# Gate and up of the layer-1 feed-forwards by Strassen's seven products, with all sums on VectorE

## Chip, core and metric

The kernel runs on one core of a Trainium2 chip. The metric is the device time of one execution in microseconds (us). Its engines are TensorE (PE, with weight loads shown as PEld), VectorE (DVE), ScalarE (ACT), GpSimd (POOL) and SyncE (SP, which only issues transfers here). All engines run at once, each through its own instructions in order; semaphores tie them together.

## The reference

One inference step of a trunk of two layers, in float32, for 528 prompt tokens (512 and 16 meta tokens) and 8 sample tokens, that is 536 columns. The width is 1024 and the feed-forward has 2816 hidden units:

```python
def swiglu(h, w_gu, w_down):
    gate, up = jnp.split(h @ w_gu, 2, axis=-1)
    return (jax.nn.silu(gate) * up) @ w_down
...
for l in range(DEPTH):
    xp = xp + 0.5 * swiglu(rmsnorm(xp, norm_g[l, 0]), ffn1_w_gu[l], ffn1_w_down[l])
    ...
    xp = xp + mp
    xs = xs + ms
    xp = xp + 0.5 * swiglu(rmsnorm(xp, norm_g[l, 2]), ffn2_w_gu[l], ffn2_w_down[l])
```

Here mp and ms are the mixer's outputs for the rows normalised with norm_g[l, 1]; the samples xs go through the feed-forwards as the prompt xp does. The mixer of layer 0 is a convolution module beside windowed attention; that of layer 1 is a grouped complex state-space model (SSM) with a gated linear projection (glu).

## The kernel before

Activations lie with the model width on the partitions: eight residual tiles `x[0]` to `x[7]` of [128, 536], in two halves of 268 columns (264 prompt tokens and 4 samples). Every product is made from exact parts: a factor is split into a high part, rounded to the format in which PE takes four-byte numbers in one pass, and the low part that is left. `weights` (L116 and on) loads a [128, 8, 128] block into `raw` (four buffers) on SP's queue, ACT copies it to `whi` (L126) and DVE subtracts to get `wlo` (L127), three buffers each. `gemm` (L137, L140) runs whi x xh, whi x xl and wlo x xh for eight rows of tiles and two halves: 48 matmuls of 268 columns.

`ffn` takes the 22 tiles of the hidden width in blocks of 8, 8 and 6. For each tile there are a gate product and an up product, 96 matmuls, into PSUM tiles `mm` and `S`. Then DVE scales gate by `R`, the reciprocal root mean square (L273), ACT takes silu (L274), DVE scales up (L275) and multiplies (L276), and ACT and DVE split the outcome into `mh` and `ml` (L146, L147). After a block the down products follow, eight of 48 (or 36) matmuls, each added to its residual tile by DVE (L288). In the last block `finalize` also makes the scaled parts `xh` and `xl` of each residual tile for the next stage (L155, L156) and adds up its squares (L162, L163); `rstd` sums the squares over the partitions by a product with ones (L185) and takes the root (L172 to L177).

The preparation of the SSM, `ssm_prep`, needs no token. It is a generator of 54 steps, one of which is drawn after each tile of the feed-forward up to the last two of a block, and after each of the first six down products: 34 steps lie in the second feed-forward of layer 0 and 20 in the first of layer 1. Its steps hold DVE work (L736 to L742, L898 to L905), some small products, ACT copies (L889, L923) and transfers to scratch on POOL's queue. The order on each engine is made by a scheduler from the dependences and the order in the program, so an engine's row is not simply the program's.

## Time and profile before

| | |
|---|---|
| time, median of 3 runs | 2066.57 us (2066.05 to 2070.46) |
| span of the profiled execution | 2071.1 us (its time around the span isn't told apart) |
| PE busy | 2023.6 us, 98% |
| DVE busy | 1133.5 us, 55% |
| ACT busy | 644.8 us, 31% |
| chain that ended last | PE 91%, DVE 5% |
| mean granted clock of PE | 0.989 of full |

By stage the profiled execution divides so: load of tokens and first feed-forward up to 262 us, mixer of layer 0 to 665, its second feed-forward to 1058, first feed-forward of layer 1 to 1450, SSM mixer to 1560, glu to 1675, second feed-forward of layer 1 with the end to 2071. In the page "idle before" a group of operations is the time its engine stood still ahead of them, with the one that ended it. A group's mean is over the whole span unless a stretch is named.

### The profile page before, as it was taken

To read this page: it belongs to the slowest core of one execution; us is meant where nothing else is said; L and a number is where in the kernel's file an instruction comes from. 1 tells how busy PE (TensorE), PEld (TensorE's weight loads), DVE (VectorE), ACT (ScalarE), POOL (GpSimd) and SP (SyncE) were. 2 spreads that over 40 slices of the span, in tenths; PEclk is the share of its full clock that TensorE was granted. 3 is DMA by queue.
4 is the path that set the end of the run, shared out by engine and by line. 5 is a ranking of instruction groups with operands and counts; after the bars stand their busy time and mean duration, and the time that the engine had idled before them with its cause. 6 is when DMAs were issued, how large, how long until landed. Compare 5 with 4: busy or idle time off the path is not lost.

```text
span 2071.1 us, 37762 instructions
## 1 busy us (share of the span) xinstructions
PE 2023.6 (98%) x16302; PEld 1981.4 (96%) x16302; DVE 1133.5 (55%) x1819; ACT 644.8 (31%) x970; POOL 114.4 (6%) x172
## 2 busy tenths in 40 slices
PE   6999999999999999999999999999989999999998
PEld 5999999998779999999999999999989999999998
DVE  4443434479967874655575544345784444344336
ACT  3322222333446322322242222123324332122223
POOL 2000000012200000000010000000110000000000
PEclk9999999999979999999999999999999999999999
DMA  6432332232005343344344433623682323332321
GB/s 174 113 100 84 91 92 86 79 84 52 27 19 129 112 129 92 105 122 115 97 133 121 119 109 109 181 81 91 185 256 77 92 87 88 92 92 83 91 77 57
DMA packets 371494, 213.51 MB, mean 103 GB/s; under 512 B 36119, under 2 KB 362323, under 8 KB 370921
## 3 DMA queue, kind: packets, MB, share of 16 engines
q1 hardware_dynamic: 354897, 190.63, 32.1%
q0 software_dynamic: 5872, 19.40, 3.1%
q8 instruction: 128, 2.10, 0.4%
q10 hardware_dynamic: 10560, 1.09, 0.4%
q14 instruction: 37, 0.30, 0.0%
HBM read 193.14 MB, written 23.65 MB: 105 GB/s over the span
## 4 chain that ended last, share of the span: by engine, by line
PE 91%; DVE 5%; DMA 1%; ACT 1%; issue 1%; SPq 1%; ACTq 0%; DVEq 0%
PE mm L137 39%; PE mm L140 19%; PE S L137 18%; PE S L140 9%; DVE yc L425 1%; PE S L598 1%; DVE wlo L127 1%; DMA raw<-in_ffn_w_gu 1%; PE ms L606 0%; PE ms L887 0%; DMA mC<-dC 0%; PE ms L612 0%; DVE Sc L1029 0%; SPq L203 0%; PE ms L919 0%
## 5 line engine op out<-in xcount | busy, mean ns | idle before, releaser
L126 ACT ACTIVATE whi<-raw 128x1024 fp32r<-128x1024 f32 (+2 forms) x324 | 329.5, 1017 | 1138.9 <-PE mm L137 533.5
L137 PE MATMUL mm<-xh,whi 128*128 128x268 f32 x2144 | 445.2, 289 | 7.4 <-DVE tb L406 2.6
L137 PE MATMUL mm<-xl,whi 128*128 128x268 f32 x2144 | 442.1, 287 | 0.0
L140 PE MATMUL mm<-xh,wlo 128*128 128x268 f32 x2144 | 441.6, 287 | 0.0
L127 DVE TENSOR_TENSOR wlo<-raw,whi 128x1024 fp32r<-128x1024 f32 (+2 forms) x324 | 381.1, 1177 | 67.7 <-ACT whi L126 59.8
L137 PEld LDWEIGHTS mm<-xh,whi 128*128 128x128 f32 x2144 | 335.0, 189 | 10.2 <-DVE tb L406 3.0
L137 PEld LDWEIGHTS mm<-xl,whi 128*128 128x128 f32 x2144 | 336.2, 189 | 1.1 <-issue 0.5
L140 PEld LDWEIGHTS mm<-xh,wlo 128*128 128x128 f32 x2144 | 335.1, 188 | 2.0 <-issue 1.7
L137 PE MATMUL mm<-mh,whi 128*128 128x268 f32 x1216 | 258.6, 290 | 1.9 <-DVE xl L156 1.1
L140 PE MATMUL mm<-mh,wlo 128*128 128x268 f32 x1216 | 256.3, 287 | 0.8 <-DVE wlo L127 0.8
L137 PE MATMUL mm<-ml,whi 128*128 128x268 f32 x1216 | 256.4, 288 | 0.0
L137 PE MATMUL S<-xh,whi 128*128 128x268 f32 x1024 | 212.3, 288 | 2.6 <-DVE us L985 2.6
L137 PE MATMUL S<-xl,whi 128*128 128x268 f32 x1024 | 210.3, 287 | 0.0
L140 PE MATMUL S<-xh,wlo 128*128 128x268 f32 x1024 | 210.1, 287 | 0.0
L137 PEld LDWEIGHTS mm<-mh,whi 128*128 128x128 f32 x1216 | 193.2, 190 | 3.5 <-ACT whi L126 2.1
L140 PEld LDWEIGHTS mm<-mh,wlo 128*128 128x128 f32 x1216 | 192.9, 189 | 1.5 <-DVE wlo L127 1.0
L137 PEld LDWEIGHTS mm<-ml,whi 128*128 128x128 f32 x1216 | 193.7, 190 | 0.4 <-issue 0.2
L137 PEld LDWEIGHTS S<-xh,whi 128*128 128x128 f32 x1024 | 160.4, 189 | 3.1 <-issue 2.9
L137 PEld LDWEIGHTS S<-xl,whi 128*128 128x128 f32 x1024 | 160.6, 189 | 0.1
L140 PEld LDWEIGHTS S<-xh,wlo 128*128 128x128 f32 x1024 | 160.0, 189 | 0.0
L275 DVE TENSOR_TENSOR tb<-mm,R 128x536 f32<-128x536 f32 x60 | 43.0, 717 | 193.5 <-PE mm L140 193.1
L288 DVE SCALAR_TENSOR_TENSOR x<-mm,x 128x536 f32<-128x536 f32 x59 | 42.2, 716 | 163.1 <-PE mm L140 163.1
(455 smaller groups left out, 2203.3 us busy)
## 6 DMA issues: line engine op xcount, KB each, us to landing
raw<-in_ffn_w_gu SPq DMA_DIRECT2D x174, 512.0 KB
raw<-in_ffn_w_down SPq DMA_DIRECT2D x64, 512.0 KB
raw<-in_ffn_w_down SPq DMA_DIRECT2D x32, 384.0 KB
raw<-in_ssm_w_glu SPq DMA_DIRECT2D x16, 512.0 KB
raw<-in_ab_w_in SPq DMA_DIRECT2D x10, 512.0 KB
dC<-CL POOLq DMA_DIRECT2D x32, 128.0 KB, 3.0
dB<-B POOLq DMA_DIRECT2D x8, 512.0 KB, 3.5
dT<-dK POOLq DMA_DIRECT2D x8, 512.0 KB, 4.9
```

The source lines that it names most:

```text
L126: nc.scalar.activation(hi[:, :K], raw[:, :K], AF.Copy)
L127: nc.vector.tensor_sub(lo[:, :K], raw[:, :K], hi[:, :K].bitcast(F32))
L137: nc.tensor.matmul(ps[:, h, :HT], hi[:, k, :], src[:, h * HT:(h + 1) * HT], start=(k == 0 and i == 0), stop=False)
L140: nc.tensor.matmul(ps[:, h, :HT], lo[:, k, :], xh[k][:, h * HT:(h + 1) * HT], start=False, stop=(k == K - 1))
L275: nc.vector.tensor_mul(halves(b[:]), pu[:, :, :HT], R)
L288: nc.vector.scalar_tensor_tensor(x, ps[:, :, :HT], 0.5, x, op0=OP.mult, op1=OP.add)
L425: nc.vector.scalar_tensor_tensor(y, z, wcol(c, j), y, op0=OP.mult, op1=OP.add)
L598: nc.tensor.matmul(S[:, g, :w], qT[t][rw, 128 * b:128 * b + 128], kT[rw, k0:k0 + w], start=False, stop=True)
```

## The change

In the two feed-forwards of layer 1, gate and up of a tile are computed together. The input is seen as two halves of the width (tiles 0 to 3 and 4 to 7) by two halves of the tokens, the weights as two halves of the width by gate and up, and the two-by-two product of blocks is made by the seven products of Strassen in Winograd's form. Each product P1 to P7 is 4 rows of tiles x 3 parts = 12 matmuls of 268 columns, so 84 for a tile where there were 96.

- `operands` (called by `finalize` for the input of these two feed-forwards) makes the sums of input blocks and splits each into parts: `xh`, `xl` hold scaled tiles or differences, `eh`, `el` and `fh`, `fl` further combinations.
- `seven_weights` loads gate (G) and up (U), makes the sums S, q and G + U with DVE (L230, L231, L233, L235 of the changed kernel) and splits G, U, S and the half-sized q: ACT at L226, DVE at L227. `DMASUM` is off.
- `seven` orders the products by the table `SLOTS`, so that products of two neighbouring tiles alternate. PSUM sums the products that share a bank; the rest goes by ACT copies out of PSUM (sn at L272 and L278, u3 at L280, tb at L284) and DVE sums of 268 columns (L276, L281, L286). Then come R, silu, R, the product and the split (L287 to L290, L148, L149).
- The SSM preparation, and that of mixer 0, is drawn two steps at a slot, so that the SSM's lies wholly in the second feed-forward of layer 0. `then` closes its pool and opens the pool `fx` of the new tiles ahead of the last down products; `glu` becomes a function of its own, so that `fx` can be opened between the SSM mixer and glu.

The removed comments are left out of the diff.

```diff
+SLOTS = dict(P1=0, P2=1, P6=3, P5=5, P7=6, P4=9, P3=11)
+STRASSEN, DMASUM = (3, 5), False
...
-        if g < 6:
+        if g in STRASSEN:
+            self.operands(d, col)
+        elif g < 6:
...
+    def extra(self, pool):
+        self.fx = pool
+        t = lambda n, w: pool.tile([128, w], F32R, name=n)
+        self.eh, self.el = ([t(f"{n}{k}", NT) for k in range(4)] for n in ("eh", "el"))
+        self.fh, self.fl = ([t(f"{n}{k}", HT) for k in range(4)] for n in ("fh", "fl"))
+    def operands(self, d, col):
+        nc, k = self.nc, d % 4
+        x, l, r = self.x[d], slice(0, HT), slice(HT, NT)
+        t = lambda n, bufs=1: self.fx.tile([128, NT], F32, name=n, bufs=bufs)
+        if d < 4:
+            if d == 0:
+                self.b12 = [self.fx.tile([128, HT], F32, name=f"b12{i}") for i in range(4)]
+                self.t1 = [self.fx.tile([128, NT], F32, name=f"t1{i}") for i in range(4)]
+            w, b = self.t1[k], self.b12[k]
+            nc.scalar.activation(w[:, l], x[:, l], AF.Copy, scale=col)
+            nc.scalar.activation(b[:], x[:, r], AF.Copy, scale=col)
+            nc.vector.tensor_sub(w[:, r], w[:, l], b[:])
+            self.put(self.xh[d][:], self.xl[d][:], w[:])
+            return
+        w, b = self.t1[k], self.b12[k]
+        u, e, f = t("ou"), t("oe"), self.fx.tile([128, HT], F32, name="of")
+        nc.scalar.activation(u[:], x[:], AF.Copy, scale=col)
+        self.put(self.xh[d][:], self.xl[d][:], u[:])
+        nc.vector.scalar_tensor_tensor(e[:, l], w[:, r], -1.0, u[:, r], op0=OP.mult, op1=OP.subtract)
+        nc.vector.tensor_sub(e[:, r], u[:, r], b[:])
+        self.put(self.eh[k][:], self.el[k][:], e[:])
+        nc.vector.scalar_tensor_tensor(f[:], e[:, l], -1.0, u[:, l], op0=OP.mult, op1=OP.subtract)
+        self.put(self.fh[k][:], self.fl[k][:], f[:])
+    def seven_weights(self, gu, f):
+        nc = self.nc
+        k0, k1 = slice(0, 4), slice(4, 8)
+        G, gh, gl = self.wtiles()
+        U, uh, ul = self.wtiles()
+        S = self.fx.tile([128, 8, 128], F32, name="sraw")
+        sh, sl = (self.wts.tile([128, 8, 128], F32R, name=n, bufs=3) for n in ("whi", "wlo"))
+        q = self.fx.tile([128, 4, 128], F32, name="sq4")
+        qh, ql = (self.fx.tile([128, 4, 128], F32R, name=n) for n in ("qh", "ql"))
+        g, u = gu[:, :, f:f + 128], gu[:, :, D_FF + f:D_FF + f + 128]
+        nc.sync.dma_start(G[:], g)
+        if DMASUM:
+            nc.sync.dma_start(S[:, k1], u[:, k1])
+            nc.sync.dma_start(U[:], u)
+            nc.gpsimd.dma_start(S[:, k1], u[:, k0], accum_op=OP.add)
+            nc.gpsimd.dma_start(U[:, k0], g[:, k0], accum_op=OP.add)
+        else:
+            nc.sync.dma_start(U[:], u)
+        def split(h, l, r):
+            nc.scalar.activation(h[:], r[:], AF.Copy)
+            nc.vector.tensor_sub(l[:], r[:], h[:].bitcast(F32))
+        split(gh, gl, G)
+        if not DMASUM:
+            nc.vector.tensor_add(S[:, k1], U[:, k0], U[:, k1])
+        nc.vector.tensor_add(S[:, k0], S[:, k1], G[:, k0])
+        split(sh, sl, S)
+        nc.vector.tensor_add(q[:], S[:, k0], G[:, k1])
+        if not DMASUM:
+            nc.vector.tensor_add(U[:, k0], U[:, k0], G[:, k0])
+        split(uh, ul, U)
+        split(qh, ql, q)
+        l, r = slice(0, HT), slice(HT, NT)
+        X = lambda t, c: [a[:, c] for a in t]
+        x0, x1 = slice(0, 4), slice(4, 8)
+        return {"P1": (gh, gl, 0, X(self.xh[:4], l), X(self.xl[:4], l)),
+                "P2": (gh, gl, 4, X(self.xh[4:], l), X(self.xl[4:], l)),
+                "P3": (qh, ql, 0, X(self.xh[4:], r), X(self.xl[4:], r)),
+                "P4": (uh, ul, 4, X(self.fh, l), X(self.fl, l)),
+                "P5": (sh, sl, 4, X(self.xh[:4], r), X(self.xl[:4], r)),
+                "P6": (sh, sl, 0, X(self.eh, l), X(self.el, l)),
+                "P7": (uh, ul, 0, X(self.eh, r), X(self.el, r))}
+    def seven(self, gu, f0, nf):
+        nc = self.nc
+        l, r = slice(0, HT), slice(HT, NT)
+        st, zs = {}, None
+        for n, p in sorted(((n, p) for n in range(nf) for p in SLOTS), key=lambda a: 7 * a[0] + SLOTS[a[1]]):
+            if p == "P1":
+                if n % 2 == 0:
+                    zs = self.scores()
+                w = self.seven_weights(gu, (f0 + n) * 128)
+                st[n] = dict(w=w, xy=self.acc2(), z=zs[:, n % 2], sn=self.fx.tile([128, NT], F32, name="sn", bufs=2),
+                             u3=self.fx.tile([128, HT], F32, name="u3"), a=self.work("ta"), b=self.work("tb"))
+            s = st[n]
+            X, Y, Z = s["xy"][:, 0, :HT], s["xy"][:, 1, :HT], s["z"][:, :HT]
+            ps, first, last = {"P1": (X, 1, 0), "P2": (Z, 1, 1), "P6": (X, 0, 0), "P5": (Y, 1, 0), "P7": (X, 0, 0),
+                               "P4": (X, 0, 1), "P3": (Y, 0, 1)}[p]
+            hi, lo, c, bh, bl = s["w"][p]
+            for k in range(4):
+                for i, (w, b) in enumerate(((hi, bh), (hi, bl), (lo, bh))):
+                    nc.tensor.matmul(ps, w[:, c + k, :], b[k], start=bool(first and k + i == 0),
+                                     stop=bool(last and k == 3 and i == 2), skip_group_check=True)
+            sn, u3, a, b = s["sn"], s["u3"], s["a"], s["b"]
+            if p == "P1":
+                nc.scalar.activation(sn[:, l], X, AF.Copy)
+                if f0 + n == 0:
+                    self.rstd()
+            elif p == "P2":
+                nc.vector.tensor_add(a[:, l], sn[:, l], Z)
+            elif p == "P6":
+                nc.scalar.activation(sn[:, r], X, AF.Copy)
+            elif p == "P7":
+                nc.scalar.activation(u3[:], X, AF.Copy)
+                nc.vector.tensor_add(b[:, r], u3[:], Y)
+            elif p == "P4":
+                nc.scalar.activation(b[:, l], X, AF.Copy)
+            elif p == "P3":
+                nc.vector.tensor_add(a[:, r], sn[:, r], Y)
+                nc.vector.tensor_mul(a[:], a[:], self.R[:])
+                nc.scalar.activation(a[:], a[:], AF.Silu)
+                nc.vector.tensor_mul(a[:], a[:], self.R[:])
+                nc.vector.scalar_tensor_tensor(b[:], b[:], -1.0, a[:], op0=OP.mult, op1=OP.mult)
+                self.put(self.mh[n][:], self.ml[n][:], b[:])
+                del st[n]
...
-    def ffn(self, wgu, wdn, gnext, filler=None, fin=None, head=None):
+    def ffn(self, wgu, wdn, gnext, filler=None, fin=None, head=None, seven=None, then=None):
         nc, tc = self.nc, self.tc
         gu = wgu.rearrange("(k p) f -> p k f", p=128)
         R = halves(self.R[:])
         for f0, nf in ((0, 8), (8, 8), (16, 6)):
-            for i in range(nf):
+            if seven:
+                self.seven(gu, f0, nf)
+            for i in range(0 if seven else nf):
                 f = (f0 + i) * 128
                 if f or not head:
                     pg = self.acc()
...
                 self.put(self.mh[i][:], self.ml[i][:], b[:])
                 if filler is not None and i < nf - 2:
                     next(filler, None)
+                    next(filler, None)
             dn = wdn[f0 * 128:(f0 + nf) * 128].rearrange("(k p) f -> p k f", p=128)
-            if f0 == 16 and fin is not None:
-                self.down_last(fin, dn, nf)
-                return
+            if f0 == 16:
+                if seven:
+                    seven.close()
+                if then:
+                    then()
+                if fin:
+                    with tc.tile_pool(name="fin", bufs=1) as p:
+                        self.down_last(p, dn, nf)
+                    return
             for d in range(ND):
                 ps = self.acc()
                 self.gemm(ps, self.weights(dn[:, :, d * 128:(d + 1) * 128], nf), self.mh[:nf], self.ml[:nf])
...
                 nc.vector.scalar_tensor_tensor(x, ps[:, :, :HT], 0.5, x, op0=OP.mult, op1=OP.add)
                 if f0 == 16:
                     self.finalize(d, gnext)
-                if filler is not None and d < 6:
+                if filler is not None and d < 6 and f0 < 16:
                     next(filler, None)
+                    next(filler, None)
...
-    def mixer1(self, gnext):
+    def mixer1(self, gnext, then):
         with self.tc.tile_pool(name="m1", bufs=1) as p:
-            self._mixer1(p, gnext)
-    def _mixer1(self, p, gnext):
+            self._mixer1(p)
+        then()
+        self.glu(gnext)
+    def _mixer1(self, p):
...
+    def glu(self, gnext):
+        nc, io = self.nc, self.io
...
-        with tc.tile_pool(name="sp", bufs=1) as sp:
-            prep = self.ssm_prep(sp)
-            self.ffn(io["ffn2_w_gu"][0], io["ffn2_w_down"][0], 3, prep)
-            self.ffn(io["ffn1_w_gu"][1], io["ffn1_w_down"][1], 4, prep)
+        sp, fx = ExitStack(), ExitStack()
+        prep = self.ssm_prep(sp.enter_context(tc.tile_pool(name="sp", bufs=1)))
+        def then():
             self.finish(prep)
-        self.mixer1(5)
-        with tc.tile_pool(name="fin", bufs=1) as p:
-            self.ffn(io["ffn2_w_gu"][1], io["ffn2_w_down"][1], None, fin=p)
+            sp.close()
+            self.extra(fx.enter_context(tc.tile_pool(name="fx", bufs=1)))
+        self.ffn(io["ffn2_w_gu"][0], io["ffn2_w_down"][0], 3, prep, then=then)
+        self.ffn(io["ffn1_w_gu"][1], io["ffn1_w_down"][1], 4, seven=fx)
+        fx = ExitStack()
+        self.mixer1(5, lambda: self.extra(fx.enter_context(tc.tile_pool(name="fx", bufs=1))))
+        self.ffn(io["ffn2_w_gu"][1], io["ffn2_w_down"][1], None, fin=True, seven=fx)
```

Three places show how the order moves. On DVE, in the middle of the first feed-forward of layer 1, one tile was this (S and mm are PSUM tiles):

```order
L273 TENSOR_TENSOR ta<-mm,R 128x536
L127 TENSOR_TENSOR wlo<-raw,whi 128x1024
L275 TENSOR_TENSOR tb<-S,R 128x536
L276 TENSOR_TENSOR tb<-tb,ta 128x536
L127 TENSOR_TENSOR wlo<-raw,whi 128x1024
L147 TENSOR_TENSOR ml_111<-tb,mh_103 128x536
```

and now most of one tile is this, with L289, L230 and L290 behind it to close the round:

```order
L227 TENSOR_TENSOR wlo<-raw,whi 128x1024
L231 TENSOR_TENSOR sraw<-sraw,raw 128x512
L235 TENSOR_TENSOR raw<-raw 128x512
L276 TENSOR_TENSOR ta<-sn,S 128x268
L227 TENSOR_TENSOR wlo<-raw,whi 128x1024
L149 TENSOR_TENSOR ml_112<-tb,mh_104 128x536
L286 TENSOR_TENSOR ta<-sn,mm 128x268
L227 TENSOR_TENSOR ql<-sq_12020,qh 128x512
L287 TENSOR_TENSOR ta<-ta,R 128x536
L227 TENSOR_TENSOR wlo<-sraw,whi 128x1024
L233 TENSOR_TENSOR sq_12149<-sraw,raw 128x512
L281 TENSOR_TENSOR tb<-u_12039,mm 128x268
```

The gate and up splits of 1024 columns have become three, and the sums of weights and of products stand between them, for different tiles.

On ACT at the same place the row was:

```order
L126 ACTIVATE whi<-raw 128x1024
L274 ACTIVATE ta<-ta 128x536
L126 ACTIVATE whi<-raw 128x1024
L146 ACTIVATE mh_103<-tb 128x536
L126 ACTIVATE whi<-raw 128x1024
```

and now, for one tile:

```order
L226 ACTIVATE whi<-raw 128x1024
L272 ACTIVATE sn<-mm 128x268
L226 ACTIVATE whi<-raw 128x1024
L284 ACTIVATE tb<-mm 128x268
L148 ACTIVATE mh_105<-tb 128x536
L278 ACTIVATE sn<-mm 128x268
L226 ACTIVATE qh<-sq_12149 128x512
L226 ACTIVATE whi<-sraw 128x1024
L280 ACTIVATE u_12168<-mm 128x268
L288 ACTIVATE ta<-ta 128x536
```

The copy of P1's bank (sn, L272) stands behind the high part of the next weights, and three more copies out of PSUM (L284, L278, L280) stand among the splits.

On DVE at the end of the feed-forward before (second of layer 0), where the last residual tile x_84 is finished and its parts are made:

```order
L288 SCALAR_TENSOR_TENSOR x_83<-mm,x_83 128x536
L127 TENSOR_TENSOR wlo<-raw,whi 128x1024
L156 SCALAR_TENSOR_TENSOR xl_99<-x_83,gcols,xh_91 128x536
L288 SCALAR_TENSOR_TENSOR x_84<-S,x_84 128x536
L163 TENSOR_TENSOR sq<-sq,ta 128x536
L127 TENSOR_TENSOR wlo<-raw,whi 128x1024
L156 SCALAR_TENSOR_TENSOR xl_100<-x_84,gcols,xh_92 128x536
L163 TENSOR_TENSOR sq<-sq,ta 128x536
```

and now, the end of this row (x_84 is written eleven rows ahead of the first one shown):

```order
L149 TENSOR_TENSOR el_10920<-oe,eh_10916 128x536
L233 TENSOR_TENSOR sq_11506<-sraw,raw 128x512
L149 TENSOR_TENSOR fl_10928<-of,fh_10924 128x268
L201 SCALAR_TENSOR_TENSOR oe<-t_10981,ou 128x268
L202 TENSOR_TENSOR oe<-ou,b_10977 128x268
L303 TENSOR_TENSOR tb<-ta 128x268 x2
L204 SCALAR_TENSOR_TENSOR of<-oe,ou 128x268
L149 TENSOR_TENSOR xl_100<-ou,xh_92 128x536
L304 SCALAR_TENSOR_TENSOR tb<-ms,tb 128x268 x2
L149 TENSOR_TENSOR el_10921<-oe,eh_10917 128x536
L149 TENSOR_TENSOR fl_10929<-of,fh_10925 128x268
L305 TENSOR_SCALAR tb<-tb 128x268 x2
```

The low part xl_100 stood three rows behind x_84, and now stands eighteen behind it; the parts el and fl of tile 7, and the roots of the norm (L303 to L305), lie around it.

## Rows read from the trace of the kernel before

**Rows 1.** The page: busy time by engine, and the chain that ended last.

```profile
PE 2023.6 (98%) x16302; PEld 1981.4 (96%) x16302; DVE 1133.5 (55%) x1819; ACT 644.8 (31%) x970; POOL 114.4 (6%) x172
...
PE 91%; DVE 5%; DMA 1%; ACT 1%; issue 1%; SPq 1%; ACTq 0%; DVEq 0%
```

**Rows 2.** Busy us by stage: length, each engine with its count, granted clock, DMA.

```profile
26.00:262.00 236.00, 232.55 (x1861) 229.49 (x1860) 107.95 (x145) 71.16 (x90) 13.72 (x28) 1.00 0.38 110
...
665.00:1058.00 393.00, 393.00 (x3220) 391.31 (x3220) 245.63 (x475) 113.62 (x146) 24.28 (x45) 1.00 0.39 113
1058.00:1450.00 392.00, 392.00 (x3208) 390.13 (x3208) 189.75 (x245) 111.42 (x140) 17.99 (x35) 1.00 0.40 115
...
1675.00:2071.00 396.00, 387.92 (x3142) 387.14 (x3140) 172.31 (x260) 107.81 (x148) 2.98 (x3) 0.99 0.29 83
```

**Rows 3.** Timeline inside the last feed-forward: start, duration, engine, line, operation, count.

```profile
1704.22 0.42 PE L137 MATMUL mm<-xh,whi 128*128 128x268 f32 x2
1704.23 1.06 ACT L126 ACTIVATE whi<-raw 128x1024 fp32r<-128x1024 f32 x1 [3.52 <-PE S L137]
...
1705.19 0.63 ACT L274 ACTIVATE ta<-ta 128x536 f32<-128x536 f32 x1
...
1710.16 0.42 PE L137 MATMUL mm<-xh,whi 128*128 128x268 f32 x2
```

**Rows 4.** DVE's groups by line and shape: count, busy us, mean ns, idle before.

```profile
L127 DVE TENSOR_TENSOR wlo<-raw,whi 128x1024 fp32r<-128x1024 f32 x276 | 339.6, 1231 | 67.0 <-ACT whi L126 59.2
...
L127 DVE TENSOR_TENSOR wlo<-raw,whi 128x512 fp32r<-128x512 f32 x16 | 10.8, 681 | 0.6 <-ACT whi L126 0.5
...
L174 DVE TENSOR_TENSOR tb<-ta 128x268 f32<-128x268 f32 x14 | 5.9, 437 | 3.3 <-ACT ta L172 3.2
```

**Rows 5.** Timeline of DVE at operations that stand in a queue.

```profile
1196.51 1.22 DVE L127 TENSOR_TENSOR wlo<-raw,whi 128x1024 fp32r<-128x1024 f32 x1
1197.64 0.69 DVE L740 TENSOR_TENSOR w<-bb,pw 128x512 f32<-128x512 f32 x1
1198.24 0.69 DVE L741 TENSOR_TENSOR w<-bb,pw 128x512 f32<-128x512 f32 x1
1198.96 0.69 DVE L742 TENSOR_TENSOR Z<-w,w 128x512 f32<-128x512 f32 x1
...
1220.48 0.72 DVE L276 TENSOR_TENSOR tb<-tb,ta 128x536 f32<-128x536 f32 x1
1221.11 1.22 DVE L127 TENSOR_TENSOR wlo<-raw,whi 128x1024 fp32r<-128x1024 f32 x1
```

**Rows 6.** ACT's groups by line and shape, whole span.

```profile
L126 ACT ACTIVATE whi<-raw 128x1024 fp32r<-128x1024 f32 x276 | 292.5, 1060 | 1044.0 <-PE mm L137 493.0 <-issue 312.1 <-PE S L137 238.9
L146 ACT ACTIVATE mh<-tb 128x536 fp32r<-128x536 f32 x88 | 57.5, 653 | 74.9 <-DVE tb L276 74.7
...
L126 ACT ACTIVATE whi<-raw 128x512 fp32r<-128x512 f32 x16 | 10.0, 624 | 10.9 <-PE mm L140 5.0 <-PE mm L137 4.9 <-DMA craw<-in_ssm_c_re 1.0
...
L146 ACT ACTIVATE mh<-yc 128x268 fp32r<-128x268 f32 x8 | 3.1, 412 | 0.0
```

**Rows 7.** PE's groups from 1058 to 1450 us: the sum over squares.

```profile
L185 PE MATMUL ms<-sq,ones 128*128 128x268 f32 x4 | 1.1, 389 | 0.0
```

**Rows 8.** Timeline of DVE, then ACT, at the start of layer 1.

```profile
1060.22 0.72 DVE L288 SCALAR_TENSOR_TENSOR x<-S,x 128x536 f32<-128x536 f32 x1 [0.64 <-PE S L140]
...
1062.61 0.77 DVE L156 SCALAR_TENSOR_TENSOR xl<-x,gcols,xh 128x536 fp32r<-128x536 f32 x1
1063.30 0.71 DVE L163 TENSOR_TENSOR sq<-sq,ta 128x536 f32<-128x536 f32 x1
...
1067.97 1.28 ACT L172 ACT_TABLE_LOAD   x1
1069.26 0.86 ACT L172 ACTIVATE ta<-ms,eps 128x268 f32<-128x268 f32 x2
```

## The prediction, made before the changed kernel ran

> **What bounds the kernel now.** I read the busy shares and the chain of work that ended last first [rows 1]: TensorE (PE) is busy for 98% of the span and holds 91% of the chain, VectorE (DVE) is busy for 55%, ScalarE (ACT) for 31%. Then the busy time by stage [rows 2]. In the feed-forwards around the change PE is busy for 393.00 of 393 us, 392.00 of 392 and 387.92 of 396, at a granted clock of 1.00, 1.00 and 0.99 (the upper of its two levels, 2.4 GHz). DVE is busy there for 245.63, 189.75 and 172.31 us. So a matmul less in these stages is time less, as long as DVE and ACT don't become later than PE. Last the pace of PE: one weight tile of 48 matmuls starts at 1704.22 and the next at 1710.16 [rows 3], 5.94 us, or 123.75 ns a matmul. A feed-forward tile (gate and up) takes 11.88 us.
>
> **What the change takes from PE.** A tile of a layer-1 feed-forward has 7 x 12 = 84 matmuls in place of 96, of the same 268 columns: 84 x 0.12375 = 10.395 us. There are 22 tiles in each of two feed-forwards: 44 x 12 x 0.12375 = **65.3 us less**, if PE never waits.
>
> **What it puts on DVE.** Per tile: three 1024-column subtractions (low parts of G, U, S), five 512-column operations (the four sums of weights and the low part of q), three 268-column sums from PSUM, three plain 536-column operations (two products with R, the low part of mh) and one fused one. The durations are 1231, 681 and 437 ns for the first three forms [rows 4], 0.72 us for a 536-column one [rows 5]. But operations that are queued start before the one ahead has ended: 1.13 us after a 1024-column start (1196.51 to 1197.64), 0.60 after a 512-column one (1197.64 to 1198.24), 0.63 after a 536-column one (1220.48 to 1221.11) [rows 5], 0.69 after a fused one (1062.61 to 1063.30) [rows 8]. For 268 columns no such pair is at hand; 437 less the same 80 ns is about 0.36 (an estimate; between 0.36 and 0.44). Sum: 3 x 1.13 + 5 x 0.60 + 3 x 0.36 + 3 x 0.63 + 0.69 = **10.05 us a tile**, against PE's 10.395. DVE goes from half idle to 97% busy; it fits by 0.35 us, with nothing to spare for a wait. With whole durations in place of starts the sum is 3 x 1.231 + 5 x 0.681 + 3 x 0.437 + 3 x 0.72 + 0.77 = 11.34 us, the other bound.
>
> The pair 1198.24 to 1198.96 [rows 5] shows when the whole duration counts: an operation that needs the result of the one ahead starts 0.72 us after it, not 0.60. In the new order consecutive DVE operations mostly belong to different tiles or products.
>
> The Trainium skill, VectorE: DVE Perf Modes, "The DRAIN you can't avoid", says more: that the next operation does not start until the pipe of the one ahead is empty, waits or not. By that rule a tile would cost DVE the whole durations, and the change would be worth little; it is the third rival below. The starts above disagree with it for operations that don't depend on each other.
>
> **What it puts on ACT.** Per tile three copies of 1024 columns (1060 ns), one of 512 (624), four of 268 columns from PSUM (no such row; the nearest, 268 columns from SBUF, 412), silu and mh (0.63 and 653) [rows 3, 6]: 3 x 1.06 + 0.62 + 4 x 0.41 + 0.63 + 0.65 = 6.72 us of 10.4. ACT has room, but it works strictly in order, and PE now waits for it inside a tile: the product P6 adds to the bank of P1 and must follow the copy of that bank. Between the end of P1 and the start of P6 stands one product, 12 x 0.12375 = 1.485 us. In the order of ACT the copy stands behind the high part of U of the next tile, which reuses a buffer whose last reader is P1 itself. Before, such a copy starts at 1704.23, 0.01 us after the next product (1704.22), where the last two matmuls of a product no longer read the buffer [rows 3]; now only the last one doesn't, so the copy starts 0.12 later, 0.13 us into the next product. So 0.13 + 0.96 (1704.23 to the silu behind it at 1705.19 [rows 3]) + 0.41 + some hundredths for the signal = 1.55, and PE waits 0.07 us. P4 waits for DVE's sum tb (L281 of the changed kernel) and P2 for its sum ta (L276) and the low part of G, all in the queue that is 97% full; I add 0.10, a choice (from 0 to the 0.95 of the other bound). **T = 10.395 + 0.17 = 10.57 us** a tile: 44 x 0.17 = 7.5 us back. Bounds: no wait (T = 10.40), and DVE by whole durations (T = 11.34).
>
> **What it puts at the starts.** Before, the last residual tile of layer 0 is written at 1060.22 and its low part at 1062.61, 2.4 us later; the tile before had given the matmuls enough to do, and PE lost nothing [rows 8, 2]. Now `operands` builds four more parts for each of the tiles 4 to 7, and 18 DVE operations start between x_84 and xl_100, weight sums among them: after x_84's own 0.69 four of 512 columns (4 x 0.60), one of 1024 (1.13), ten of 268 (10 x 0.36), three of 536 (3 x 0.63). That is 9.7 us; with 0.2 for the signal from PE and xl's own 0.72, xl_100 is there 10.6 us after the end of the last down product, and el_10921, three operations on, after 11.9. ACT puts the table load and the reciprocal roots (1.28 + 0.86 [rows 8]) ahead of xh_92, and these wait for the ones product (4 matmuls, 1.1 us [rows 7]) and with it for the last square, which stands in the same DVE queue; that chain comes to the same 10 us. PE has 36 matmuls (4.46 us) and the ones product for this time, so it loses 11.9 - 5.6 = 6.3 us, and I put 2.2 on top for the weights of the next tile, which DVE reaches only then: 8.5 us, with 7 and 14 as bounds (no backlog and all of 5 operations of 1.13 late). At the second layer-1 feed-forward the glu tiles take 11.88 us of PE each (2 x 5.94), so DVE enters without a backlog: 4 us (3 to 6).
>
> **Block edges.** Each feed-forward has three blocks. At an edge the products of the first tile find empty queues, and the last tile's chain from R to ml (0.72 + 0.63 + 0.72 + 0.77 + 0.65 + 0.71 [rows 3, 5, 6, 8], 4.2 us) is hidden by seven eighths of a down product (0.875 x 5.94 = 5.2 us). I put 0.7 us on each of six: 4 us, 0 to 8.
>
> **The preparation moved.** All its steps, two at a slot, now lie in the second feed-forward of layer 0. There DVE had 393 - 245.63 = 147 us free [rows 2]. Drawn on the last feed-forward, which holds no step (172.31), the 34 steps of this stage cost 73 us of DVE, 2.2 each, and the 20 in the next one (189.75) 17 us, 0.9 each. The 20 moved steps so add 17 to 43 us, and DVE reaches at most 289 of 393. Their work on PE moves with them, zero in sum. The transfers that they issue on POOL's queue lie beside 24.28 us of POOL work in 393 [rows 2]. A down tile with two steps brings DVE to about 6.2 us against PE's 5.94 for some tiles in a row, so I put 2 us, with 0 and 10 as bounds. For the preparation of mixer 0, drawn two steps at a slot too, DVE has 236 - 108 = 128 us free [rows 2]: nothing.
>
> Sum: -65.3 + 7.5 + 8.5 + 4 + 4 + 2 = **-39.3 us**. The span of the profiled execution, 2071.1, stands 4.5 us above the median of the runs (2066.57) and 0.6 above the slowest of them. 2071.1 - 39.3 = 2031.8 in such an execution; against the median **2027 us**.
>
> **The rivals**, with F = 8.5 + 4 + 4 + 2 = 18.5 us of fixed costs and 44 x (11.88 - T) of gain:
> - *DVE sets the pace with its waits.* At 97% each wait at the head of its queue (the low part of U waits for the end of P1, mh and silu come from ACT) is lost for good. With one wait of 0.9 us a tile, T = 11.0: 38.7 - 18.5 = -20, **2046 us**. For it: in the page of before, DVE waits for ACT's high parts in 59.2 us of 276 cases [rows 4], 0.2 us each. Against: the queue holds work of three tiles. Chance 0.2.
> - *The weights are late.* whi and wlo have three buffers, just one tile's three weights. If each tile's split had to wait for the product that frees its buffer and PE had to wait for the split, then 1.06 (ACT) + 1.23 (DVE) + 0.2 of signals, 2.5 us, would lie on the path of each tile: T = 12.9, +44.9 + 18.5 = +63, **2130 us**. It is slower from T = 11.88 - 18.5/44 = 11.46 on, that is, once 1.07 us of the 2.5 is uncovered. Against: each buffer is freed at the end of P1, P4 or P5 and the next tile's product on it is five or more products (some 7 us) away. Chance 0.08.
> - *Whole durations on DVE.* T = 11.34: 23.8 - 18.5 = -5, **2061 us**. Against it are the starts of [rows 5]. Chance 0.1.
> - *No waits, filled starts.* T = 10.40 and half of F: -65.1 + 9 = -56, **2011 us**. Chance 0.12.
>
> **How the numbers follow.** Forecast 0.5. The range leaves out the late weights and a part of the whole durations, and reaches down to the case without waits: 2010 to 2056. About 0.2% of the time (4 us) is what a measurement of this kernel can tell from no change. The chance of faster than 2062.4 is 0.5 + 0.2 + 0.12 + half of 0.1, 0.87; same 0.05; slower 0.08.
>
> **What would show it.** In the profile after: 84 matmuls of the product line per 10.4 to 10.7 us in a layer-1 feed-forward; DVE above 93% busy there; PE's idle time mostly behind ACT's copy sn; a gap of 7 to 14 us in PE at the start of the first layer-1 feed-forward, behind xl and el of DVE, and a smaller one at the second; PE without gaps in the second feed-forward of layer 0. The prediction is wrong if the tile pitch is above 11 us, if PE waits for DVE's low parts in each tile, or if the preparation shows as idle PE in layer 0.

## The result and the profile after

The changed kernel takes **2037.2 us** (median of 4 runs, 2035.6 to 2040.2), against 2068.5 for the kernel before in the same session: a ratio of 0.9843, 95% interval 0.9825 to 0.9861, or 31 us less. The forecast was 2027, the range 2010 to 2056. The profiled execution has a span of 2038.4 us, 32.7 less than the 2071.1 of before.

The page, in answer to [rows 1]: busy time by engine, then the chain that ended last.

```profile
PE 1978.1 (97%) x15774; PEld 1924.3 (94%) x15774; DVE 1378.6 (68%) x2263; ACT 790.1 (39%) x1274; POOL 113.5 (6%) x172
...
PE 89%; DVE 6%; ACT 2%; DMA 1%; issue 1%; SPq 1%; ACTq 0%; DVEq 0%
```

PE has exactly 528 instructions less (16302 before), VectorE (DVE) 444 more. PE still holds the chain. Its busy time fell by 45.5 us, not by the 65.3 of 528 matmuls in a full queue, and its idle time rose by 12.8 (47.5 to 60.3). Busy time alone doesn't say where; the stages do. Each column below is the time between two matmul starts of the trace: the last down product of one stage to that of the next, and the last one to the end of the span ("tail").

| us | second ffn of layer 0 | first ffn of layer 1 | mixer 1 | second ffn of layer 1 | tail |
|---|---|---|---|---|---|
| before | 400.6 | 399.6 | 202.1 | 398.5 | 11.0 |
| after | 407.7 | 378.1 | 201.4 | 376.2 | 16.5 |
| difference | +7.0 | -21.5 | -0.7 | -22.3 | +5.5 |

The preparation's own matmuls moved from the stage in the second column to that in the first (by e1 below, -6.9 and +7.0). So Strassen gave 14.6 us in the first layer-1 feed-forward and 22.3 in the second, of 32.7 each, and 5.5 us went at the end; another 0.7 lies in the stages ahead of these. The same by windows, in answer to [rows 2] (length, then each engine's busy us and count in the order PE, PEld, DVE, ACT, POOL, then granted clock, DMA share, GB/s): first the steady part of the first layer-1 feed-forward, then its start in two pieces.

```profile
1230.00:1290.00 60.00, 59.52 (x476) 58.92 (x475) 55.73 (x83) 34.58 (x56) 0.00 (x0) 1.00 0.35 103
...
1066.40:1080.00 13.60, 7.55 (x41) 5.80 (x40) 12.95 (x27) 9.60 (x16) 0.00 (x0) 0.93 0.13 39
1080.00:1085.00 5.00, 5.00 (x23) 4.84 (x23) 2.52 (x6) 1.35 (x3) 0.00 (x0) 0.52 0.36 107
```

In the steady part PE is busy for 99% and DVE for 93%: both nearly full, as forecast. At the start DVE is busy for 12.95 of 13.6 us and PE for 7.55: there PE works at DVE's pace. In the next 5 us PE runs without a gap but starts only 23 matmuls (40 at 123.75 ns): the granted clock is 0.52, the lower of its two levels (1.2 GHz), after a stretch in which PE had been idle for 6 of 13.6 us.

What PE waited for in the whole of that feed-forward (1066 to 1450): the instruction that waited, the one waited for, us in total, times, the longest.

```profile
PE S L268 <- ACT xh L148: 2.7, 1, 2.7
PE mm L268 <- ACT sn L278: 1.4, 3, 0.5
PE ms L314 <- DVE sq L167: 1.2, 1, 1.2
PE S L268 <- DVE xl L149: 0.8, 1, 0.8
PE mm L268 <- issue: 0.7, 1, 0.7
PE mm L139 <- DVE ta L286: 0.6, 1, 0.6
PE mm L268 <- DVE el L149: 0.5, 1, 0.5
```

Five of these seven (xh, sq, xl, issue, el; 5.9 us) lie in the first 14 us. The wait for ACT's copy sn comes three times in 22 tiles, once a block, not in each tile. The pitch of a tile is read from the first matmul of its product P3, for tiles 4 to 7 of the first block, the second of these four left out; ahead of them the products are ordered otherwise, and P3 starts 5.7 to 13.4 us apart (start, duration, instruction):

```profile
1123.32 0.39 PE L268 MATMUL mm<-xh,qh 128*128 128x268 f32 x1
...
1144.48 0.29 PE L268 MATMUL mm<-xh,qh 128*128 128x268 f32 x1
1155.19 0.39 PE L268 MATMUL mm<-xh,qh 128*128 128x268 f32 x1
```

1123.32 to 1155.19 is three tiles: **10.62 us a tile** (forecast 10.57; 11.88 before).

The critical part of the start, in order of time: DVE writes the last residual tile, ACT can scale it (ou) only six microseconds later, then come the table load and the roots, then xh, for which PE waits.

```profile
1067.27 0.70 DVE L428 SCALAR_TENSOR_TENSOR x<-S,x 128x536 f32<-128x536 f32 x1
...
1073.13 0.43 DVE L204 SCALAR_TENSOR_TENSOR of<-oe,ou 128x268 f32<-128x268 f32 x1
...
1073.92 0.73 ACT L199 ACTIVATE ou<-x,gcols 128x536 f32<-128x536 f32 x1
...
1074.67 1.28 ACT L301 ACT_TABLE_LOAD   x1
...
1076.71 0.65 ACT L148 ACTIVATE xh<-ou 128x536 fp32r<-128x536 f32 x1
...
1077.41 0.39 PE L268 MATMUL S<-xh,whi 128*128 128x268 f32 x1 [2.66 <-ACT xh L148]
```

The tile is ready at 1067.97, but `ou` has one buffer, and its last reader for the tile before (L204) starts at 1073.13, because DVE's queue is full until then.

The end of the span: first before, then after. Last down product, sum of squares over the ones for the first half of the tokens (after), its DMA to the output.

```profile
2060.08 0.29 PE L140 MATMUL mm<-mh,wlo 128*128 128x268 f32 x1
2060.37 0.83 SPq L1183 DMA_DIRECT2D out_y_prompt<-y  x2
```

```profile
2021.97 0.29 PE L142 MATMUL S<-mh,wlo 128*128 128x268 f32 x1
2022.42 0.73 PE L1303 MATMUL ms<-ones,sq 128*128 128x1 f32 x6
2023.43 1.28 ACT L1317 ACT_TABLE_LOAD   x1
2026.91 0.86 SPq L1327 DMA_DIRECT2D out_y_prompt<-y  x2
```

Before, the first half's rows leave 0.3 us after the last product; after, 4.9 us after it. Its norm, which was worked beside the last products, is now worked behind them.

### The profile page after: what moved, and what is told of

It is laid out like the page before. It is cut to its first block, busy times and chain, and to the rows that moved or that the text cites. A ratio compares the mean times of both kernels' runs of the same rounds, so it can differ in the third digit from the quotient of the medians.

```text
span 2038.4 us, 37681 instructions
## 1 busy us (share of the span) xinstructions
PE 1978.1 (97%) x15774; PEld 1924.3 (94%) x15774; DVE 1378.6 (68%) x2263; ACT 790.1 (39%) x1274; POOL 113.5 (6%) x172
## 4 chain that ended last, share of the span: by engine, by line
PE 89%; DVE 6%; ACT 2%; DMA 1%; issue 1%; SPq 1%; ACTq 0%; DVEq 0%
PE mm L139 28%; PE mm L268 19%; PE mm L142 14%; PE S L139 12%; PE S L142 6%; PE S L268 3%; DVE yc L566 1%; PE S L739 1%; DVE wlo L129 1%; DMA raw<-in_ffn_w_gu 1%; ACT whi L128 0%; PE ms L747 0%; PE ms L753 0%; DMA mC<-dC 0%; PE ms L1028 0%
## 5 line engine op out<-in xcount | busy, mean ns | idle before, releaser
L129 DVE TENSOR_TENSOR wlo<-raw,whi 128x1024 fp32r<-128x1024 f32 (+2 forms) x236 | 272.7, 1157 | 59.8 <-ACT whi L128 55.6
L142 PE MATMUL mm<-xh,wlo 128*128 128x268 f32 x1280 | 266.5, 289 | 0.0
L139 PEld LDWEIGHTS mm<-xh,whi 128*128 128x128 f32 x1280 | 201.8, 191 | 11.3 <-issue 3.6
L142 PEld LDWEIGHTS mm<-xh,wlo 128*128 128x128 f32 x1280 | 202.2, 190 | 2.0 <-issue 1.7
L139 PEld LDWEIGHTS mm<-xl,whi 128*128 128x128 f32 x1280 | 202.6, 191 | 1.1 <-issue 0.5
L226 ACT ACTIVATE whi<-raw 128x1024 fp32r<-128x1024 f32 x88 | 93.4, 1061 | 104.1 <-issue 42.9
L139 PE MATMUL S<-mh,whi 128*128 128x268 f32 x604 | 128.4, 288 | 0.6 <-ACT whi L128 0.6
L139 PE MATMUL S<-ml,whi 128*128 128x268 f32 x604 | 127.3, 287 | 0.0
L142 PE MATMUL S<-mh,wlo 128*128 128x268 f32 x604 | 127.2, 286 | 0.0
L227 DVE TENSOR_TENSOR wlo<-raw,whi 128x1024 fp32r<-128x1024 f32 x88 | 107.4, 1221 | 15.8 <-ACT whi L226 14.9
L268 PE MATMUL mm<-eh,whi 128*128 128x268 f32 x352 | 103.1, 293 | 0.9 <-issue 0.7
## 6 DMA issues: line engine op xcount, KB each, us to landing
raw<-in_ffn_w_down SPq DMA_DIRECT2D x32, 384.0 KB
```

The source lines that it names most:

```text
L129: nc.vector.tensor_sub(lo[:, :K], raw[:, :K], hi[:, :K].bitcast(F32))
L139: nc.tensor.matmul(ps[:, h, :HT], hi[:, k, :], src[:, h * HT:(h + 1) * HT], start=(k == 0 and i == 0), stop=False)
L142: nc.tensor.matmul(ps[:, h, :HT], lo[:, k, :], xh[k][:, h * HT:(h + 1) * HT], start=False, stop=(k == K - 1))
L226: nc.scalar.activation(h[:], r[:], AF.Copy)
L227: nc.vector.tensor_sub(l[:], r[:], h[:].bitcast(F32))
L268: nc.tensor.matmul(ps, w[:, c + k, :], b[k], start=bool(first and k + i == 0), stop=bool(last and k == 3 and i == 2), skip_group_check=True)
```

## The experiments

The stages of all kernels as in the table above, with median and ratio to the kernel before in the same session. The profiles of the same code differ by some 6.5 us ahead of these stages, in layer 0, and the SSM mixer with glu, which is not in the table, takes from 198.8 to 202.7 us. A feed-forward repeats to some tenths where its order and the granted clock at its start are the same, and is the finer measure; where that clock differs it can move by 1 to 2 us (see the end of this section).

| kernel | median | ratio, 95% | first ffn | second ffn | tail |
|---|---|---|---|---|---|
| e1 prep only | 2070.1 | 0.9996 [0.9979, 1.0012] | 392.7 | 398.5 | 11.0 |
| e2 first only | 2056.4 | 0.9943 [0.9925, 0.9962] | 378.1 | 397.8 | 15.4 |
| e3 second only | 2049.9 | 0.9913 [0.9882, 0.9945] | 392.7 | 375.1 | 16.5 |
| e4 two buffers | 2031.9 | 0.9824 [0.9796, 0.9853] | 376.0 | 376.1 | 16.4 |
| e5b early norm | 2035.4 | 0.9838 [0.9816, 0.9861] | 377.9 | 374.9 | 15.3 |
| e6 more on DVE | 2047.7 | 0.9897 [0.9877, 0.9916] | 382.9 | 380.8 | 16.3 |
| e7 sums on POOL | 2047.7 | 0.9906 [0.9881, 0.9932] | 383.2 | 383.6 | 16.4 |
| e8 e4, e5b, e7 | 2048.5 | 0.9902 [0.9882, 0.9922] | 384.0 | 382.6 | 15.3 |
| e9 e2, turned | 2054.3 | 0.9932 [0.9914, 0.9950] | 377.9 | 398.5 | 11.0 |
| e10 e4, e5b | 2033.5 | 0.9834 [0.9818, 0.9851] | 373.8 | 374.9 | 15.8 |
| e11 e10, more banks | 2030.7 | 0.9820 [0.9802, 0.9838] | 375.4 | 374.8 | 14.4 |

**The parts one by one.** The moved preparation alone, then with Strassen in one feed-forward only (the calls that build the operands go with it):

```diff
-STRASSEN, DMASUM = (3, 5), False
+STRASSEN, DMASUM = (), False      # e1;  (3,) in e2, (5,) in e3
```

> Only the move of the SSM preparation: both layer-1 feed-forwards compute gate and up as before, the preparation is drawn two steps at a slot in the second feed-forward of layer 0. Theory (the moved steps are hidden beside the matmuls, their 7 us of work on TensorE only moves): the time of the kernel before, 2068.5 within 2 us; the second feed-forward of layer 0 about 7 us longer, the first of layer 1 about 7 us shorter. Rival (the preparation overfills VectorE and POOL's queue there): 2074 to 2080 us, with idle time of TensorE in the second feed-forward of layer 0.

> Seven products in the first feed-forward of layer 1 alone, the second one as before (the preparation moved too). Theory (loss at places: 32.7 us saved at TensorE's pace, 12 given back at this start, 5.5 to 6 at the six edges and the rest): 15 us below the kernel before, 2053 to 2054 us; the end after the last down product takes 10.7 us, as before. Rival (VectorE is too full, the loss is spread over all tiles): tiles of 10.7 to 11 us instead of 10.4. Rival on the end (the changed order of the end comes from the preparation or from the accumulators' turn, not from the seven products ahead of it): the end takes 16 us here too, 2058 to 2059 us.

> Seven products in the second feed-forward of layer 1 alone, the first one as before (the preparation moved too). Theory: 32.7 us saved, 4.6 given back at its start, 5.5 to 6 at the edges and the rest, 5.4 at the end: 17 us below the kernel before, 2051 to 2052 us, and the end after the last down product takes 16 us. Rival (the end's order comes from elsewhere): the end takes 10.7 us here, 2046 us.

The preparation costs nothing: e1 is within 0.2% of before, and in its trace the second feed-forward of layer 0 grows by 7.0 us (to 407.7) and the next shrinks by 6.9. Of the two feed-forwards the first gives 13 us (15 forecast) and the second 20 (17 forecast); the sum, 33, is the change's own 31 within the intervals. On the end, e2's rival came true: its second feed-forward is the plain one, and yet its tail is 15.4 us. So the longer tail is not Strassen's work on DVE in the last block, or not that alone.

**The start.** Two buffers in place of one for `ou` and `oe`:

```diff
-        u, e, f = t("ou"), t("oe"), self.fx.tile([128, HT], F32, name="of")
+        u, e, f = t("ou", 2), t("oe", 2), self.fx.tile([128, HT], F32, name="of")
```

> The changed kernel with two buffers for ou and oe, the tiles in which the operands of a feed-forward are made. Theory A (the start of the first feed-forward waits for a chain of single buffers: ou of tile 7 is written only when the sums of tile 6 have read theirs): the 12 us of that start fall by 3 to 6 us, 2031 to 2034 us. Theory B (the length of VectorE's queue sets the start, whatever the buffers): no change, 2036 to 2038 us.

In the trace of e4, ACT scales the last tile at once, and its last parts on DVE stand here:

```profile
1063.80 0.73 ACT L199 ACTIVATE ou<-x,gcols 128x536 f32<-128x536 f32 x1
...
1069.53 0.70 DVE L149 TENSOR_TENSOR xl<-ou,xh 128x536 fp32r<-128x536 f32 x1
1070.16 0.68 DVE L233 TENSOR_TENSOR sq<-sraw,raw 128x512 f32<-128x512 f32 x1
1070.76 0.70 DVE L149 TENSOR_TENSOR el<-oe,eh 128x536 fp32r<-128x536 f32 x1
...
1071.52 0.59 PE L268 MATMUL mm<-el,whi 128*128 128x268 f32 x1 [0.71 <-DVE el L149]
```

ou now follows its tile by half a microsecond, where it was six. But xl comes only 5.7 us later, el 7.0: DVE has no gap from 1049.5 to 1071.8, and weight sums and low parts stand between the tile's parts. The wait moved from the buffer to DVE's queue, and the first feed-forward became 2.2 us shorter, not the whole start. The same code gives 4.3 us in e10 and 2.7 in e11, where less of the start falls in the lower clock. Ahead of that, at the 45th matmul behind the last down product, PE is 9.5 us late against 123.75 ns a matmul in the changed kernel, and 7.6, 7.0 and 7.7 in e4, e10 and e11: the buffers are worth about 2 us. (By medians e4 is 5 us below the changed kernel, in another session; the two intervals overlap.)

**Is DVE at its limit?** One more sum of 512 columns a tile, into a tile that nobody reads:

```diff
+        spare = self.fx.tile([128, 4, 128], F32, name="spare")
+        nc.vector.tensor_add(spare[:], S[:, k0], G[:, k1])
```

> The changed kernel with one more 512-column sum on VectorE in each tile of the layer-1 feed-forwards, whose result nobody reads. Theory (TensorE at 10.395 us a tile bounds, VectorE needs 10.05 by start-to-start durations): VectorE comes to 10.65 us, becomes the bound, tiles of 10.6 to 10.8 us; a block of 8 has a lag of some tiles to absorb, so 5 to 13 us more, 2042 to 2050 us. Rival 1 (VectorE has more room than the sum says): within 2 us of 2037. Rival 2 (VectorE already bounds, at whole durations): 0.69 us a tile, 30 us more, 2067 us.

It costs 10.5 us by medians of two sessions, and 4.8 and 4.7 us in the two feed-forwards by stages: 0.21 us of PE's time a tile for about 0.60 on DVE. PE's waits from 1100 to 1440 in e6 (line numbers two higher from here on):

```profile
PE mm L270 <- ACT sn L280: 3.0, 6, 0.6
PE mm L270 <- ACT tb L286: 1.9, 5, 0.4
PE S L139 <- ACT whi L128: 1.0, 1, 1.0
```

With the ta wait of 0.6 that is 6.5 us, where the changed kernel has 2.5 in the same stretch. PE waits for ACT's copies, not for DVE by name. The margin on DVE was below 0.6 us a tile. One thing weakens it: the scheduler's order changed with the added row, and tiles now come in pairs (P3 starts 15.7 and 6.5 us apart in turn), so a part of the 4.7 us may be the order's.

**Two sums on POOL instead.** The sums of weights at L230 and L235 move from DVE to GpSimd (POOL):

```diff
-            nc.vector.tensor_add(S[:, k1], U[:, k0], U[:, k1])
+            nc.gpsimd.tensor_add(S[:, k1], U[:, k0], U[:, k1])
...
-            nc.vector.tensor_add(U[:, k0], U[:, k0], G[:, k0])
+            nc.gpsimd.tensor_add(U[:, k0], U[:, k0], G[:, k0])
```

> The changed kernel with two of the four weight sums of a tile (U0 + U1 and G0 + U0) on GpSimd, the other two on VectorE. Theory (TensorE bounds the tiles, VectorE's queue sets the start): VectorE 8.85 us a tile, the pitch of the tiles stays at 10.4 us, and the start of the first feed-forward gets shorter by 1 to 3 us: 2033 to 2036 us. Rival (GpSimd, at about 1.8 us a sum, holds up the splits or slows VectorE): longer tiles, 2040 us or more.

10 us slower: the rival. DVE has two operations less a tile, but the others became longer. DVE's groups by line and shape from 1100 to 1400 (count, busy us, mean ns, idle before), first of the changed kernel, then of e7:

```profile
L227 DVE TENSOR_TENSOR wlo<-raw,whi 128x1024 fp32r<-128x1024 f32 x39 | 47.6, 1221 | 7.3 <-ACT whi L226 6.9
...
L290 DVE SCALAR_TENSOR_TENSOR tb<-tb,ta 128x536 f32<-128x536 f32 x19 | 13.5, 710 | 0.2
...
L231 DVE TENSOR_TENSOR sraw<-sraw,raw 128x512 f32<-128x512 f32 x19 | 13.0, 685 | 0.1
...
L281 DVE TENSOR_TENSOR tb<-u,mm 128x268 f32<-128x268 f32 x19 | 8.1, 426 | 0.0
```

```profile
L227 DVE TENSOR_TENSOR wlo<-raw,whi 128x1024 fp32r<-128x1024 f32 x37 | 50.7, 1384 | 2.3 <-ACT whi L226 2.3
L290 DVE SCALAR_TENSOR_TENSOR tb<-tb,ta 128x536 f32<-128x536 f32 x19 | 23.7, 1248 | 0.4
...
L231 DVE TENSOR_TENSOR sraw<-sraw,raw 128x512 f32<-128x512 f32 x18 | 20.0, 1112 | 8.7 <-POOL sraw L230 8.7
...
L281 DVE TENSOR_TENSOR tb<-u,mm 128x268 f32<-128x268 f32 x18 | 7.7, 425 | 0.0
```

L290 grew by 538 ns, L231 by 427, L227 by 163 on the mean; (19 x 0.538 + 18 x 0.427 + 37 x 0.163) / 19 = 1.26 us a tile, as much as the two sums had taken from start to start (2 x 0.60). L233, not shown, adds 0.15 (686 to 841 ns), and L231 waits for POOL's sum besides, 8.7 us in all. L281, which reads one operand from PSUM, kept its time. And the sum itself takes two and a half times as long on POOL (1.70 against 0.69):

```profile
1247.94 1.70 POOL L230 TENSOR_TENSOR sraw<-raw 128x512 f32<-128x512 f32 x1 [7.18 <-DVE wlo L227]
1249.72 1.65 POOL L235 TENSOR_TENSOR raw<-raw 128x512 f32<-128x512 f32 x1
```

The Trainium skill, SBUF — State Buffer, "SBUF: two separate sides", has the rule: VectorE and GpSimd share a pair of ports as an exclusive lock, held for a whole instruction, which a VectorE operation with two SBUF inputs takes and so waits for a GpSimd operation that reads SBUF. The trace agrees: of the rows above those with two inputs in SBUF became longer (L290 710 to 1248 ns), the one with an input in PSUM did not (426 and 425). It is those that ran beside POOL: over both feed-forwards of e7, the 26 rows of L290 that overlap one of POOL's sums take 1.55 us on the mean, the other 18 take 0.72, while the 22 rows of L281 that overlap one take 0.43. As in e6, tiles come in pairs here (P3 starts 16.8 and 5.8 us apart), so how much of the 5 and 7 us that the two feed-forwards lost is the order's was not separated.

**The tail.** e5b lets the first half's sum of squares go ahead of its last output rows; e9 is e2 with the counter that deals out the PSUM accumulators turned on by one; e10 is e4 and e5b together; e11 adds banks for the last rows:

```diff
-                flush(1)                               # e5b, e10, e11 (and four buffers for g)
+                flush(4 if h == 0 else 1 if d == n else 8)
...
+        self.turn = (self.turn + 1) % 3                # e9, ahead of the down products
...
-        flush(0)                                       # e11
+        while pending:
+            ps = self.acc2()
+            for b, one in enumerate(pending[:2]):
+                rows(*one, ps[:, b])
+            del pending[:2]
```

> The changed kernel, with the end rearranged: the sums of squares of the first half of the columns (early, then end of half 0) take their PSUM bank ahead of the transposes of the last tiles, and g has four buffers for it. Theory (the 5.4 us that the end lost are a place in the queue: the sums of squares of half 0 stand behind the transposes, which share two banks, and the norm of half 0 runs after the last product in place of beside it): the end after the last down product falls from 16.4 us to 11 to 13, the time to 2032 to 2034 us. Rival (the transposes and copies themselves are the limit, whatever the order): the end stays at 15 to 16.5 us, 2036 to 2038 us.

> The three edits together: two buffers for ou and oe, the early sums of squares, two weight sums on GpSimd. Theory (three separate places, so the gains add): 5.3 + 3 to 5 + 1 to 3 us below the changed kernel, 2024 to 2028 us. Rival (the places share a resource): no better than the best of the three alone, about 2032 us.

> The kernel with only the first feed-forward of layer 1 in seven products (median 2056.4 us, 15.4 us from its last down product to the end of the span), with one line more: the counter that deals out the three PSUM accumulators is turned on by one before the last down products. Theory: Strassen's feed-forward leaves out 44 calls of that counter, so the norm of the first half of the tokens asks for the accumulator that is read out last, and is computed behind the last product instead of beside it. Then the tail is 10.5 to 11.5 us, as before the change, and the median 2050.5 to 2053. Rival: the tail grew because the copies of the output rows run late. Then it stays at 15 to 15.5 us and the median at 2055 to 2058.

> The changed kernel with two buffers for the operands u and e (as e4, 2031.9 us) and the sum of the first half's norm ahead of its last output rows (as e5b, 1.1 us off the tail). Theory: the two gains lie in different places and add up: 2029.5 to 2032, tail 15 to 15.5 us, PE lag at the start of the first layer-1 feed-forward 10 to 10.5 us. Rival: the start's gain is lost later, 2033 to 2036.

> As e10, and the output rows that are still to be transposed behind the last product take their PSUM banks from the accumulators, which are free by then, two rows to one of them, beside the two small banks that rows had before. Theory: a row waits for one of two banks to be copied out (some 1.3 us a row), so the tail falls to 11.5 to 13.5 us and the median to 2026 to 2029. Rival: VectorE, which copies the rows and works the norm in the same queue, sets the pace: tail 14.5 to 16 us, median as e10 within 1 us.

e9 settles e2's tail: 11.0 us, as before the change, with the other stages within 0.7 us of e2's. The sum for the first half (L1303, bank mm), the scaling of its rows (L1325) and the last down product, in e9:

```profile
2035.16 0.72 PE L1303 MATMUL mm<-ones,s 128*128 128x1 f32 x6
...
2038.40 1.12 ACT L1325 ACTIVATE y<-y,r 128x384 f32<-128x384 f32 x2
...
2038.95 0.29 PE L142 MATMUL S<-mh,wlo 128*128 128x268 f32 x1
```

and in e2:

```profile
2039.37 0.29 PE L142 MATMUL mm<-mh,wlo 128*128 128x268 f32 x1
...
2039.49 0.73 PE L1303 MATMUL mm<-ones,s 128*128 128x1 f32 x6
```

Strassen's feed-forward takes its accumulators past the counter, so 44 turns are missing; the norm then asks for an accumulator that is still in use, and is worked behind the last product. (The median, 2054.3, is 1.3 above the forecast: by ratio e9 gains 2 us on e2, by the traces' tails 4.5; the interval of the ratio holds both.)

The counter does not explain the changed kernel's tail, though. There 88 turns are missing, which for three accumulators leaves the counter where e9 has it (44 missing, one given back), and the sum that asks for it (L1303, bank mm) starts 3.0 us ahead of the last product. It is the other sum of the first half, in a small bank (2022.42 above), that comes behind the last product; it stands behind output rows that use these banks. Moving it ahead (e5b) gives 1.2 us, not the 3 to 5 expected, and leaves the tail at 15.3, in the rival's range: the rows that it passes come later instead. Other banks for the last rows (e11) give 1.4 of the 2 to 4 expected. 3.4 us of the tail remain. DVE is busy there for 5.0 of the first 6 us behind the last product, but for 5.6 of 6 in the kernel before, with its short tail; the cause of these 3.4 us stays open.

e10 and e11 are the best versions with e4: 0.9820 for e11 against 0.9843 for the changed kernel, with intervals that overlap. e10's median, 2033.5, lies in its rival's range (the gain lost later), though its stages keep the start's gain whole and 0.7 of the tail's 1.2. By stages e11 is 6.1 us shorter than the changed kernel (2.7, 1.3 and 2.1), but the 1.3 in the second feed-forward comes with the granted clock, at work that no edit touches. The same 5 us, 9.0 behind the last product of glu, in the changed kernel and in e10:

```profile
1654.80:1659.80 5.00, 5.00 (x31) 5.00 (x30) 3.24 (x8) 1.45 (x2) 0.00 (x0) 0.66 0.36 105
...
1649.16:1654.16 5.00, 5.00 (x43) 5.00 (x42) 4.42 (x10) 1.86 (x3) 0.00 (x0) 1.00 0.35 105
```

PE's wait ahead of it is the same (1.8 us for whi); the granted clock fell behind it in the changed kernel, e3, e4, e6 and e7, and not in e5b, e8, e10 and e11, which have e5b's edit of the end in common. PE then comes out of this start 4.8 us late in the changed kernel, and 3.3 late in e10 and e11. Why it fell in some and not in others no run here shows. e8 is e10 with e7's edit: by medians the sums on POOL cost 15 us there.

## Why the prediction was right, and where it was off

- *What PE saves.* 528 matmuls less: confirmed by the count. In the steady part 476 start in 60 us, 126 ns each, against 123.75.
- *DVE's pace.* 10.05 us of 10.4, by starts in a queue: confirmed. DVE is busy for 93% of the steady part, and a tile takes 10.62 us. By whole durations in the trace of after, 3 x 1.221 + 5 x 0.685 + 3 x 0.427 + 4 x 0.711 = 11.2 us, DVE could not have kept this pitch. The prediction drew that rival's rule from the Trainium skill, VectorE: DVE Perf Modes, "The DRAIN you can't avoid", but left out how the passage goes on: "A next op that is not held starts earlier". With this sentence the trace agrees, 10.62 against 11.2.
- *Waits in a tile and at block edges.* 7.5 + 4 = 11.5 us forecast. What the two feed-forwards lost beside their starts: 32.7 - 14.6 - 11.1 = 7.0 and 32.7 - 22.3 - 4.8 = 5.6, together 12.6. The sum held, the mechanism in a tile did not: the wait for sn was worked out for each tile (0.07 us) and comes once a block, with 0.5 us by the view and 0.8 by the starts of PE; the rest of a tile's loss is pauses of about 0.1 us. So PE's idle time is not mostly behind sn, as forecast: in the whole view of the first feed-forward it is 1.4 of 8.4 us, and xh at the start alone is 2.7.
- *The start of the first layer-1 feed-forward.* Forecast 8.5 (7 to 14), measured 11.1: so much later than at 123.75 ns a matmul the 62nd matmul behind the last down product starts, the first at the upper clock again. The chain named (DVE's queue, the table load and the roots ahead of xh) was the right one; two things were missing: the single buffer `ou`, about 2 us by e4, and the lower clock behind the gap, some 2 to 3 us (23 matmuls in 5.00 us, which 2.85 would do). Together they are more than the 2.6 us that were missing: the 2.2 that the forecast put on top, for the weights of the next tile, was a choice, and no run shows it apart.
- *The start of the second.* Forecast 4, measured 4.8 by the same count, lower clock included; 3.3 in the runs in which it does not fall.
- *The preparation.* Forecast 2 (0 to 10), measured 0 (e1).
- *The end.* Nothing was forecast, 5.5 us came. The prediction put the tail at nothing without a reason: it did not follow what the new order does at the far end. Of the 5.5 us, the place of the first half's sum of squares and the banks of the last rows make 2.1 together (16.5 to 14.4 in e11); the rest stays open. This term is the largest part of the 6.6 us between -39.3 and -32.7: the end 5.5 more, the first start 2.6, the second 0.8, tiles and edges 1.1 more, the preparation 2 less, and 1.4 less in the mixer and layer 0, where nothing was forecast.
- *The rivals.* "DVE sets the pace" (T = 11.0) is what e6 comes near with 0.6 us more on DVE (two tiles in 22.2 us in the middle of a block), so it was a near thing. "The weights are late": in the steady part no wait of PE for whi of L226 is in the view; it is seen only at the second start (1.8 us).

## What to carry to other kernels

DVE went through a full queue by the distance from start to start, so the sum of those, not of the durations, told whether the work fits beside the bound. But at 93% there is nothing to hide a stage's start, where operands must be built first (11.1 and 4.8 us here), and the bounding engine can come out of that gap at half clock. Work can't be moved from DVE to POOL by counting DVE's operations alone: those with two inputs in SBUF stood still while POOL read it, and the time saved was paid back. A change that takes buffers past a shared rotation shifts every later user of it, so read the order at the far end of the program too.

## What the runs showed that was not expected

- The lower clock behind the start: 0.52 granted from 1080 to 1085 us.
- The same start of the second feed-forward, behind the same gap of PE, ran partly at the lower clock in five kernels and at the upper one in four (0.66 and 1.00 above): 1.5 us that a comparison of kernels would put down to the code.
- POOL lengthens a DVE operation at the end, too. Beside POOL's 1.88 us multiplication at the end of the changed kernel (L1333), a DVE operation of 0.35 us takes 1.18:

```profile
2022.85 0.35 DVE L1283 TENSOR_SCALAR g<-x,gcols 128x268 f32<-128x268 f32 x1
...
2027.52 1.88 POOL L1333 TENSOR_TENSOR y<-y,r 12x1024 f32<-12x1024 f32 x1 [9.18 <-DVE y L1293]
...
2028.39 1.18 DVE L1283 TENSOR_SCALAR g<-x,gcols 128x268 f32<-128x268 f32 x1
```

It stands in DVE's queue behind the last product, in which the tail is worked; the kernel before has the same (1.27 us), so it is no part of the 5.5 us. Taking it off POOL was not tried.
